# The down projection of nine pairs of row blocks by seven products instead of eight, and the second attention's weights split on ScalarE and VectorE

## The chip, the cores and the metric

The kernel runs on one core of a Trainium2 chip. The metric is the device time of one execution in microseconds, lower is better; the time before is the median of three runs.

## What is computed

Two decoder layers over 1,024 tokens of width 1,024 in float32. The first layer has differential attention, the second stick-breaking attention whose K and V come from the residual stream. Each layer ends in the same feed-forward block, and both of these are what the change touches:

```python
def swiglu(h, w_gate_up, w_down):
    gate, up = jnp.split(h @ w_gate_up, 2, axis=-1)
    return (jax.nn.silu(gate) * up) @ w_down
...
    for layer in range(DEPTH):
        h = rms_norm(x, mix_pre_g[layer])
...
        x = x + rms_norm(m, mix_post_g[layer])
        f = swiglu(rms_norm(x, ffn_pre_g[layer]), ffn_w_gate_up[layer], ffn_w_down[layer])
        x = x + rms_norm(f, ffn_post_g[layer])
```

`D_FF` is 2,816: 22 row blocks of 128, called f = 0 to 21 (`NF`). The gate and up product is 1,024 x 1,024 by 1,024 x 5,632, the down product 1,024 x 2,816 by 2,816 x 1,024.

## The kernel before

**Precision.** Every large product is made of three matmuls of 128x128 by 128x512 (`PASSES`): each operand is kept as a rounded part and a remainder, and high*high, low*high and high*low are summed in one PSUM bank. To split an operand is a copy that rounds (ScalarE, or GpSimd) and a subtraction (GpSimd or VectorE).

**Order of the work.** Coroutines ask for engines and buffers; the class `Weaver` runs them against its own table of costs and writes each engine's instructions down in the order in which they start there. `InOrder` fixes that order per engine. On the chip each engine takes its queue in this order, and each instruction waits for its semaphores, so a late one holds back all behind it on its engine. All DMAs are issued by SP, in one such queue.

**Gate and up.** `phase_ffn.gate_up` already uses seven products instead of eight for each f (`MORD`): `quad` in `loader` loads two 1,024x128 pieces of weights into `raw` tiles, forms five sums or differences on VectorE (`raw<-raw,raw`, `raw<-raw`), rounds seven operands on ScalarE (`w<-raw`) and subtracts on GpSimd (`w<-raw,w`). TensorE does 84 matmuls for each f, against `hT` tiles (four operands) and `hx` tiles (three, which `combine` makes at the phase's start). `take` adds the seven results from PSUM into four `e` tiles: eight additions on VectorE, four copies on ScalarE. `gated` applies silu on ScalarE and multiplies on VectorE (`e<-e`), and `store` writes to DRAM (`act`).

**Down.** `act_in` reads a block back into an `fa` or `fb` tile, rounds it on ScalarE and subtracts on VectorE. `row_job` loads and splits a block of `w_down`, mostly on GpSimd. `down` goes through the groups of `groups_of` (nine of two f and one of four); for each of 8 token blocks m and 2 column halves it does three matmuls per f, then one addition of the bank to an accumulator on VectorE (ScalarE copies in the first group). That is 22 x 16 x 3 = 1,056 matmuls in each layer. From the third token block of the first group on, the copies wait until all of `act` is stored (`all_stored`), since the accumulators lie in the same tiles `e`.

**Weights of the second attention.** While the first layer's feed-forward block runs, `pre_weights` takes 32 weight tiles of the second attention (24 with a gain, `bq`, `bk`, `bv`; then 8 without, `wo`), 128x1024 each, into `tr` tiles: GpSimd multiplies by the gain (`tr<-tr,gB`), ScalarE rounds, GpSimd subtracts (`tr<-tr,tr`), and both parts are stored. It paces itself with a delay of 10 us in the planner's time.

## Time and profile before

| what | us |
|---|---|
| median of three runs (2665.01 to 2668.43) | 2665.74 |
| the profiled execution | 2666.21 |
| its span in the profile | 2664.4 |

The profile is of one execution. Its span runs from the first instruction to the last; 1.8 us lie around it. The first layer's feed-forward block lies at about 606 to 1370 us of the span (gate and up to 1103, down from there), the second layer's at 1983 to the end (down from 2418). In the rows below, names of tiles stand as out<-in, PE is TensorE, DVE VectorE, ACT ScalarE, POOL GpSimd. Matmuls overlap, so the mean length of one is longer than the interval from one to the next.

### The profile page before, as it was taken

The numbers are of one execution on the slowest core, as the hardware profiler recorded it, in microseconds if no ns is written. First come the engines' busy times: TensorE is split into PE (matmuls) and PEld (weight loads), VectorE is DVE, ScalarE is ACT, GpSimd is POOL, SyncE is SP. The second block draws the span as 40 slices with busy tenths as digits, with TensorE's granted clock in tenths as the row PEclk, the third lists the DMA queues.
The fourth block names the chain that finished last, engine by engine and source line by source line (L and its number), as shares of the span: only waits on it lengthen the run. The fifth ranks groups of instructions, "written<-read, shape, count | busy, mean of one in ns | idle before, by whom it ended". The sixth has DMA issues, their size and how long they took to land. (4 is left out here: it accounts for less than half of the span.)

```text
span 2664.4 us, 36544 instructions
## 1 busy us (share of the span) xinstructions
PE 2544.4 (95%) x12771; PEld 2155.9 (81%) x12771; DVE 1824.4 (68%) x3151; ACT 1156.6 (43%) x2542; POOL 922.4 (35%) x769
## 2 busy tenths in 40 slices
PE   8999999896999999899999999999989999999998
PEld 8998999775777877688878888887777888888887
DVE  4767676865766767566668887878777655554667
ACT  4556555644433444310146555556455333332111
POOL 2111111334787878533210000000044545453321
PEclk9999999998999999999999999999999999999999
DMA  6333323442555465542253444434532232324223
GB/s 170 86 80 80 92 76 97 125 166 83 181 171 166 158 199 172 213 166 95 96 197 105 112 117 113 119 104 132 209 121 87 72 95 72 95 72 156 98 102 127
DMA packets 259256, 331.54 MB, mean 124 GB/s; under 512 B 20992, under 2 KB 179072, under 8 KB 259072
## 3 DMA queue, kind: packets, MB, share of 16 engines
q1 hardware_dynamic: 259072, 329.20, 40.1%
q8 instruction: 101, 1.65, 0.3%
q14 instruction: 83, 0.68, 0.1%
HBM read 197.67 MB, written 81.13 MB: 105 GB/s over the span
## 5 line engine op out<-in xcount | busy, mean ns | idle before, releaser
L283 PE MATMUL bank<-hT,w 128*128 128x512 f32 x3264 | 808.6, 398 | 19.6 <-POOL w L283 12.2
L283 PEld LDWEIGHTS bank<-hT,w 128*128 128x128 f32 x3264 | 607.8, 191 | 145.4 <-POOL w L283 15.3
L283 POOL TENSOR_TENSOR w<-raw,w 128x512 fp32r<-128x512 f32 (+1 forms) x343 | 537.2, 1588 | 365.6 <-ACT w L283 309.2
L283 PE MATMUL bank<-hx,w 128*128 128x512 f32 x1584 | 371.1, 392 | 11.0 <-DVE hx L283 8.8
L283 PEld LDWEIGHTS bank<-hx,w 128*128 128x128 f32 x1584 | 298.6, 189 | 76.0 <-DVE hx L283 11.5
L283 DVE TENSOR_TENSOR e<-e,bank 128x512 f32<-128x512 f32 x360 | 237.7, 682 | 168.2 <-PE bank L283 102.1
L283 PE MATMUL bank<-w,hT 128*128 128x384 f32 (+1 forms) x1728 | 346.2, 347 | 3.5 <-DVE v L283 1.1
L283 ACT CAST w<-raw 128x512 fp32r<-128x512 f32 x308 | 185.5, 621 | 337.7 <-DVE raw L283 210.3
L283 PEld LDWEIGHTS bank<-w,hT 128*128 128x128 f32 x1728 | 301.6, 190 | 14.2 <-DVE hT L283 1.5
L283 PE MATMUL bank<-w,fb 128*128 128x512 f32 x1344 | 311.5, 389 | 1.1 <-POOL w L283 1.0
L283 PEld LDWEIGHTS bank<-w,fb 128*128 128x128 f32 x1344 | 252.0, 188 | 54.3 <-POOL w L283 1.5
L283 DVE TENSOR_TENSOR e<-bank,e 128x512 f32<-128x512 f32 x224 | 152.6, 688 | 104.3 <-PE bank L283 102.0
L283 POOL MEMSET atB<- 128x128 f32 x128 | 25.3, 206 | 503.4 <-PE bank L283 498.5
L283 PE MATMUL bank<-ident,tr 128*128 128x128 f32 x1059 | 162.2, 281 | 39.1 <-DVE tr L283 20.2
L283 PE MATMUL bank<-w,fa 128*128 128x512 f32 x768 | 185.5, 396 | 8.5 <-ACT e L283 5.0
L283 PEld LDWEIGHTS bank<-ident,tr 128*128 128x128 f32 x1059 | 129.1, 144 | 70.3 <-DVE tr L283 22.9
L283 PEld LDWEIGHTS bank<-w,fa 128*128 128x128 f32 x768 | 145.7, 191 | 40.8 <-ACT e L283 6.5
L283 POOL TENSOR_TENSOR sm<-sm,nhalf 128x1 f32<-128x1 f32 (+1 forms) x72 | 57.8, 804 | 286.7 <-DVE sm L283 281.6
L283 DVE TENSOR_TENSOR raw<-raw,raw 128x512 f32<-128x512 f32 x132 | 156.8, 1195 | 0.0
L283 POOL TENSOR_SCALAR w<-raw 128x1024 fp32r<-128x1024 f32 x48 | 65.5, 1364 | 261.9 <-PE bank L283 173.6
L283 DVE TENSOR_TENSOR raw<-raw 128x512 f32<-128x512 f32 x88 | 62.4, 743 | 120.4 <-DMA raw<-in_ffn_w_gate_up_dram 117.8
L283 DVE TENSOR_TENSOR_SCAN rB<-rB,zeroB 128x512 f32<-128x512 f32 (+3 forms) x144 | 135.2, 953 | 7.2 <-ACT rB L283 6.0
(209 smaller groups left out, 3640.3 us busy)
## 6 DMA issues: line engine op xcount, KB each, us to landing
raw<-in_ffn_w_gate_up_dram SPq DMA_DIRECT2D x88, 512.0 KB, 5.2
xy<-st SPq DMA_DIRECT2D x192, 128.0 KB, 2.3
act<-e SPq DMA_DIRECT2D x88, 256.0 KB, 4.0
raw<-in_ffn_w_down_dram SPq DMA_DIRECT2D x44, 512.0 KB, 4.1
xyB<-stB SPq DMA_DIRECT2D x176, 128.0 KB, 3.9
fb<-act SPq DMA_DIRECT2D x28, 512.0 KB, 3.9
raw<-in_a_w_qkv_dram SPq DMA_DIRECT2D x96, 128.0 KB, 2.5
tr<-x SPq DMA_DIRECT2D x22, 512.0 KB, 4.3
```

Of the source, the lines that this page charges most:

```text
L283: return tc.keep_in_program_order(f(*a, **k))
```

## The change

For f = 0 to 17 (`ND`), in nine pairs, the down product is made by Strassen's seven products: a pair's two f are the two halves of the inner dimension, the token halves and the column halves are the other two. The pairs go in two groups, of five and of four (`D_GROUPS`); within a group, each of the seven products is summed over the group's pairs in four PSUM banks, and only then added to the accumulators. f = 18 to 21 stay as they were, as the last group.

- `pair_ops` (new) runs while gate and up goes on: five sums or differences of 128x512 on VectorE for each pair, and seven stores to DRAM (`op`) in place of four (`act`).
- `act_in` reads each of the 63 activation operands back into half a tile's width, rounds (ScalarE) and subtracts (VectorE).
- `move_weights` copies 18 blocks of `w_down` from DRAM to DRAM (`wd`). `QuarterJob` loads quarters of them into pieces of the `hT` tiles, which are lent as the last f of gate and up is done with them. `OpJob` makes the 63 weight operands: a sum or difference on VectorE for five of seven (`raw<-hT,hT`), a rounding on ScalarE, a subtraction on GpSimd.
- `down` no longer waits for the pools of its phase before the first matmul; its `evac` does.
- `pre_weights` starts 25 us later, is paced by 13.5 instead of 10 us, and does without GpSimd: for the 24 tiles with a gain eight scaled copies of 128x128 on ScalarE and eight multiply-subtracts of 128x128 on VectorE, for the 8 others a subtraction on VectorE.
- `quad` subtracts one of its seven operands (i = 2) on VectorE.

```diff
 LAMBDA_INIT = 0.8 - 0.6 * math.exp(-0.3 * 0)
 PASSES = ((0, 0), (1, 0), (0, 1))
 MORD = (3, 5, 4, 2, 6, 7, 1)
+DORD = (2, 5, 3, 4, 7, 6, 1)
+D_GROUPS = ((0, 1, 2, 3, 4), (5, 6, 7, 8))
+ND = 18
 NE = 3
...
                 g_ev, g = job.gain()
                 yield g_ev
-                v3 = raw.t.rearrange("p (c n) -> p c n", c=NC)
-                yield POOL(1024, 1.7)
-                pool.tensor_tensor(v3, v3, g.unsqueeze(2).broadcast_to([P, NC, P]), op=ALU.mult)
             h = hi.t.bitcast(F32R)
-            yield ACT(1024)
-            act.copy(h, raw.t)
+            if job.gain is not None:
+                for c in range(NC):
+                    cs = slice(c * P, c * P + P)
+                    yield ACT(P, 1)
+                    act.activation(h[:, cs], raw.t[:, cs], AF.Copy, scale=g[:, c:c + 1])
+                for c in range(NC):
+                    cs = slice(c * P, c * P + P)
+                    yield DVE(P + 58)
+                    dve.scalar_tensor_tensor(raw.t[:, cs], raw.t[:, cs], g[:, c:c + 1], hi.t[:, cs],
+                                             op0=ALU.mult, op1=ALU.subtract)
...
-            yield POOL(1024, 2.2)
-            pool.tensor_tensor(raw.t, raw.t, hi.t, op=ALU.subtract)
...
             sp.dma_start(out=job.view(raw.t), in_=job.src)
             yield delay(2.6)
             W.spawn(work(job, raw, hi), 60, "pre" + job.name)
-            yield delay(10.0)
+            yield delay(13.5)
     def loader():
         queue = []
...
-                pool.tensor_tensor(lo, src, f32(hi), op=ALU.subtract)
+                if i == 2:
+                    yield DVE(512)
+                    dve.tensor_tensor(lo, src, f32(hi), op=ALU.subtract)
+                else:
+                    yield POOL(512, 2.2)
+                    pool.tensor_tensor(lo, src, f32(hi), op=ALU.subtract)
                 job.t[i] = t
                 W.set(job.ev[i])
                 W.set(left)
...
+        def operand(k_, job):
+            yield turn[k_]
+            t = yield acq(S_w)
+            sc = None
+            if len(job.parts) == 2:
+                sc = yield acq(S_raw)
+            W.set(turn[k_ + 1])
+            W.set(job.began)
+            for x in job.parts:
+                yield x.ev
+            src = f32(job.parts[0].t.t)
+            if sc is not None:
+                yield DVE(512)
+                dve.tensor_tensor(sc.t[:, :512], src, f32(job.parts[1].t.t), op=job.op)
+                for x in job.parts:
+                    x.used()
+                src = sc.t[:, :512]
+            hi, lo = t.t[:, :512], t.t[:, 512:]
+            yield ACT(512)
+            act.copy(hi, src)
+            yield POOL(512, 2.2)
+            pool.tensor_tensor(lo, src, f32(hi), op=ALU.subtract)
+            if sc is not None:
+                W.put(sc)
...
-        st.d = [row_job(w_down[layer][f * P:(f + 1) * P], name=f"d{f}") for f in range(NF)]
...
+        for g in D_GROUPS:
+            qs = {p: {} for p in g}
+            for i in DORD:
+                for p in g:
+                    q = qs[p]
+                    if i in (2, 5, 3, 4):
+                        key = {2: 11, 5: 22, 3: 12, 4: 21}[i]
+                        f, ch = 2 * p + key // 10 - 1, key % 10 - 1
+                        q[key] = QuarterJob(st.wd[f][:, ch * 512:(ch + 1) * 512], st.wd_ev[f],
+                                            4 if key in (11, 22) else 2)
+                    parts, op = {2: ((11,), None), 5: ((22,), None), 3: ((12, 22), sub), 4: ((21, 11), sub),
+                                 7: ((21, 22), add), 6: ((11, 12), add), 1: ((11, 22), add)}[i]
+                    st.o[p, i] = OpJob([q[k] for k in parts], op, f"d{p}_{i}", began)
+        st.d = {f: row_job(w_down[layer][f * P:(f + 1) * P], after=began, name=f"d{f}")
+                for f in range(ND, NF)}
...
+        def move_weights():
+            for f in range(ND):
+                yield SP(1.0)
+                sp.dma_start(out=st.wd[f], in_=st.wd_src[f])
+                yield delay(6.0)
+                W.set(st.wd_ev[f])
+                yield delay(6.0)
+
+        def lend_q():
+            def cut(t):
+                return [t[:, k] for k in range(4)]
+
+            yield from W.lend(S_h, S_q, 8, cut, book)
+
...
+            def pair_ops(p):
+                yield pair_ev[p]
+                a11, a21, a12, a22 = gt[2 * p, 0], gt[2 * p, 1], gt[2 * p + 1, 0], gt[2 * p + 1, 1]
+                pr = plan("p.storexf" + nm, 0)
+                keep = [Ref([x], 2) for x in (a11, a22)]
+                for i, x, k in ((3, a11, keep[0]), (4, a22, keep[1])):
+                    W.spawn(store_op(p, i, x.t, k.done), pr, "storeo")
+                for i, x, y in ((2, a21, a22), (5, a11, a12), (1, a11, a22)):
+                    z = yield acq(S_sg, S_tr)
+                    yield DVE(512)
+                    dve.tensor_tensor(z.t[:, :512], x.t, y.t, op=ALU.add)
+                    W.spawn(store_op(p, i, z.t[:, :512], lambda z=z: W.put(z)), pr, "storeo")
+                for i, x, y, k in ((6, a21, a11, keep[0]), (7, a12, a22, keep[1])):
+                    yield DVE(512)
+                    dve.tensor_tensor(x.t, x.t, y.t, op=ALU.subtract)
+                    k.done()
+                    W.spawn(store_op(p, i, x.t, lambda x=x: W.put(x)), pr, "storeo")
...
+            def fin_op(k, t):
+                yield ACT(512)
+                act.copy(t.t[:, :512], f32(t.t[:, 512:]))
+                yield DVE(512)
+                dve.tensor_tensor(t.t[:, 512:], f32(t.t[:, 512:]), f32(t.t[:, :512]), op=ALU.subtract)
+                op_t[k] = t
+                W.set(op_ev[k])
+
+            for k in keys:
+                yield op_stored[k]
+                t = yield acq(S_act)
+                yield SP(0.8)
+                sp.dma_start(out=f32(t.t[:, 512:]), in_=opd[k[0]][k[1]])
+                yield delay(2.4)
+                W.spawn(fin_op(k, t), plan("p.mul" + nm, 1), "opin")
...
+            touched = {r: Ev(4) for r in (0, 1)}
+            evac_done = Ev(4 * 7 * len(D_GROUPS))
+            goes = {1: ((0, 0, 1), (1, 1, 1)), 2: ((1, 0, 1), (1, 1, -1)), 3: ((0, 1, 1), (1, 1, 1)),
+                    4: ((0, 0, 1), (1, 0, 1)), 5: ((0, 0, -1), (0, 1, 1)), 6: ((1, 1, 1),), 7: ((0, 0, 1),)}
+
+            def evac(bk, m, i, first):
+                yield dn_open
+                yield all_stored
+                for r, c, sg in goes[i]:
+                    av = acc[4 * r + m][:, c * 512:(c + 1) * 512]
+                    if first:
+                        yield ACT(512)
+                        if sg > 0:
+                            act.copy(av, bk.t)
+                        else:
+                            act.activation(av, bk.t, AF.Copy, scale=-1.0)
+                    else:
+                        yield touched[r]
+                        yield DVE(512)
+                        dve.tensor_tensor(av, av, bk.t, op=ALU.add if sg > 0 else ALU.subtract)
+                W.put(bk)
+                if first:
+                    W.set(touched[goes[i][0][0]])
+                W.set(evac_done)
+
+            for g in D_GROUPS:
+                for i in DORD:
+                    yield op_ev[g[0], i]
+                    yield st.o[g[0], i].ev
+                    bks = []
+                    for m in range(4):
+                        bks.append((yield acq(B_mm, B_sc, B_tp, B_pv)))
+                    for p in g:
+                        yield op_ev[p, i]
+                        yield st.o[p, i].ev
+                        a, w = op_t[p, i], st.o[p, i].t
+                        for m in range(4):
+                            yield PE(3)
+                            for k, (ah, wh) in enumerate(PASSES):
+                                pe.matmul(bks[m].t, a.t[:, ah * 512 + m * P:ah * 512 + (m + 1) * P],
+                                          w.t[:, wh * 512:(wh + 1) * 512],
+                                          start=(p == g[0] and k == 0), stop=(p == g[-1] and k == 2))
+                        W.put(a, w)
+                    for m in range(4):
+                        W.spawn(evac(bks[m], m, i, g == D_GROUPS[0] and i in (2, 5)), plan("p.acc" + nm, 2), "evac")
+            yield evac_done
+            W.unlend(book)
+            for gr in (list(range(ND, NF)),):
```

**VectorE in the middle of the first layer's gate and up.** `e,bank` rows are the additions from PSUM, `raw` rows the sums of weights, `e<-e` the multiplication after silu; the line is that of the recording helper, 283 before and 286 now. Before, one f and the start of the next:

```order
L283 TENSOR_TENSOR e2_5510<-e2_5510,bank6_139 128x512
L283 TENSOR_TENSOR e2_5510<-e2_5510,bank5_138 128x512
L283 TENSOR_TENSOR raw2_127<-raw0_125,raw2_127 128x512
L283 TENSOR_TENSOR e2_5510<-e2_5510,bank0_133 128x512
L283 TENSOR_TENSOR raw0_125<-raw0_125,raw2_127 128x512
L283 TENSOR_TENSOR e2_5510<-e2_5510,bank0_133 128x512
L283 TENSOR_TENSOR e2_5510<-e2_5510,bank1_134 128x512
L283 TENSOR_TENSOR raw0_125<-raw0_125,raw2_127 128x512
L283 TENSOR_TENSOR e2_5510<-e2_5510,bank4_137 128x512
L283 TENSOR_TENSOR e2_5510<-e2_5510,bank2_135 128x512 x2
L283 TENSOR_TENSOR e2_5510<-e2_5510 128x512 x2
```

In the changed kernel, as far into the stage:

```order
L286 TENSOR_TENSOR w3_119<-raw0_125,w3_119 128x512
L286 TENSOR_TENSOR raw2_127<-raw0_125,raw2_127 128x512
L286 TENSOR_TENSOR e2_5591<-e2_5591,bank5_138 128x512
L286 SCALAR_TENSOR_TENSOR tr1_129<-tr1_129,gB_103,tr0_128 128x128
L286 TENSOR_TENSOR e2_5591<-e2_5591,bank0_133 128x512
L286 TENSOR_TENSOR raw0_125<-raw0_125,raw2_127 128x512
L286 TENSOR_TENSOR e2_5591<-e2_5591,bank0_133 128x512
L286 SCALAR_TENSOR_TENSOR tr1_129<-tr1_129,gB_103,tr0_128 128x128 x2
L286 TENSOR_TENSOR e2_5591<-e2_5591,bank1_134 128x512
L286 TENSOR_TENSOR raw0_125<-raw0_125,raw2_127 128x512
L286 SCALAR_TENSOR_TENSOR tr1_129<-tr1_129,gB_103,tr0_128 128x128 x3
L286 TENSOR_TENSOR e2_5591<-e2_5591,bank4_137 128x512
```

Between the rows of one f there now stand the subtraction `w3<-raw0,w3` of a weight operand and groups of the 128x128 multiply-subtracts of `pre_weights`; the sums of `pair_ops` (`e<-e,e`) follow behind every second f.

**TensorE where the first layer's gate and up ends.** `hT` and `hx` rows are gate and up, rows with `fa` the down projection. Before, its last rows of gate and up and the first of down:

```order
L283 MATMUL bank1_134<-hx4_6094,w8_124 128x512 x2
L283 MATMUL bank1_134<-hx5_6095,w8_124 128x512
L283 MATMUL bank1_134<-hx4_6094,w8_124 128x512
L283 MATMUL bank7_140<-w0_116,fa0_6083 128x512
L283 MATMUL bank7_140<-w0_116,fa1_6084 128x512
L283 MATMUL bank7_140<-w1_117,fa0_6083 128x512
L283 MATMUL bank7_140<-w2_118,fa2_6085 128x512
L283 MATMUL bank7_140<-w2_118,fa3_6086 128x512
L283 MATMUL bank7_140<-w3_119,fa2_6085 128x512
L283 MATMUL bank6_139<-w0_116,fa0_6083 128x512
```

In the changed kernel, within the last f, where its fourth product (bank4) has begun:

```order
L286 MATMUL bank4_137<-hT6_114,w5_121 128x512
L286 MATMUL bank4_137<-hT7_115,w5_121 128x512
L286 MATMUL bank4_137<-hT6_114,w5_121 128x512
L286 MATMUL bank6_139<-w0_116,fa0_6164 128x512 x3
L286 MATMUL bank5_138<-w0_116,fa0_6164 128x512 x3
L286 MATMUL bank0_133<-w0_116,fa0_6164 128x512 x3
L286 MATMUL bank1_134<-w0_116,fa0_6164 128x512 x3
```

And 10 rows on, where gate and up goes on in the same bank:

```order
L286 MATMUL bank5_138<-w3_119,fa3_6167 128x512 x3
L286 MATMUL bank0_133<-w3_119,fa3_6167 128x512 x3
L286 MATMUL bank1_134<-w3_119,fa3_6167 128x512 x3
L286 MATMUL bank4_137<-hT6_114,w5_121 128x512
L286 MATMUL bank4_137<-hT7_115,w5_121 128x512
L286 MATMUL bank4_137<-hT6_114,w5_121 128x512 x2
```

The first four pairs of the first down product, 48 matmuls, now stand inside the last f of gate and up, ahead of three and a half of its seven products. In the second layer they stand behind the last row of gate and up.

**VectorE in the second group of the first layer's down projection.** Rows with `bank` are additions from PSUM, `fa` and `fb` rows the remainders of activation operands, `raw<-hT,hT` the sums of quarters of weights, `tr` a tile of `pre_weights`. Before, in the middle of that layer's down projection:

```order
L283 TENSOR_TENSOR acc0_8956<-bank0_133,acc0_8956 128x512
L283 TENSOR_TENSOR acc0_8956<-bank1_134,acc0_8956 128x512
L283 TENSOR_TENSOR acc1_8957<-bank7_140,acc1_8957 128x512
L283 TENSOR_TENSOR fb1_8961<-fb1_8961,fb0_8960 128x1024
L283 TENSOR_TENSOR fb3_8963<-fb3_8963,fb2_8962 128x1024
L283 TENSOR_TENSOR acc1_8957<-bank6_139,acc1_8957 128x512
L283 TENSOR_TENSOR e0_5508<-bank5_138,e0_5508 128x512
L283 TENSOR_TENSOR e0_5508<-bank0_133,e0_5508 128x512
L283 TENSOR_TENSOR e0_5508<-bank1_134,e0_5508 128x512
```

In the changed kernel:

```order
L286 TENSOR_TENSOR e0_5589<-e0_5589,bank3_136 128x512
L286 TENSOR_TENSOR e0_5589<-e0_5589,bank7_140 128x512
L286 TENSOR_TENSOR e1_5590<-e1_5590,bank4_137 128x512
L286 TENSOR_TENSOR e1_5590<-e1_5590,bank2_135 128x512
L286 TENSOR_TENSOR fb2_9461<-fb2_9461 128x512
L286 TENSOR_TENSOR e2_5591<-e2_5591,bank3_136 128x512
L286 TENSOR_TENSOR e2_5591<-e2_5591,bank7_140 128x512
L286 TENSOR_TENSOR raw2_127<-hT5_113,hT7_115 128x512
L286 TENSOR_TENSOR fb3_9462<-fb3_9462 128x512
L286 TENSOR_TENSOR raw1_126<-hT5_113,hT7_115 128x512
L286 TENSOR_TENSOR raw0_125<-hT5_113,hT7_115 128x512
L286 TENSOR_TENSOR tr2_130<-tr2_130,tr4_132 128x1024
```

Before, sixteen additions stood between one pair of remainders and the next; now eight additions for a product have between them and the next eight four or five remainders of 128x512 and three or four sums of quarters.

## Rows read from the trace of the kernel before

**Rows 1.** The head of the page, and of its DMA issues one row (KB each, us to landing).

```profile
span 2664.4 us, 36544 instructions
...
act<-e SPq DMA_DIRECT2D x88, 256.0 KB, 4.0
```

**Rows 2.** Busy time of each engine by stretch (first column), granted clock, DMA.

```profile
680.00:794.00 114.00, 114.00 (x503) 94.33 (x502) 75.59 (x84) 50.03 (x83) 86.25 (x50) 1.00 0.56 180
794.00:1046.00 252.00, 236.70 (x1011) 192.26 (x1010) 172.72 (x187) 103.14 (x176) 204.08 (x119) 0.97 0.53 174
...
1103.00:1112.00 9.00, 9.00 (x41) 7.42 (x40) 7.36 (x8) 2.84 (x5) 8.13 (x5) 1.00 0.65 223
1112.00:1130.00 18.00, 9.45 (x26) 6.23 (x26) 4.90 (x4) 9.01 (x13) 4.08 (x2) 0.75 0.74 275
...
2018.00:2418.00 400.00, 400.00 (x1767) 331.20 (x1766) 226.18 (x315) 152.28 (x269) 209.32 (x147) 1.00 0.30 92
2418.00:2657.00 239.00, 239.00 (x1056) 197.85 (x1055) 154.78 (x215) 41.61 (x68) 61.56 (x38) 1.00 0.33 113
```

**Rows 3.** Who PE waited for, first layer, 606 to 1130 us.

```profile
PE bank L283 <- POOL w L283: 12.2, 7, 2.5
...
PE bank L283 <- DVE hx L283: 7.6, 3, 2.9
PE bank L283 <- ACT e L283: 5.0, 2, 2.9
PE bank L283 <- ACT acc L283: 3.5, 1, 3.5
...
PE bank L283 <- ACT hx L283: 2.2, 1, 2.2
```

**Rows 4.** The same, second layer, 1983 to 2664 us.

```profile
PE bank L283 <- DVE hx L283: 1.2, 2, 0.7
```

**Rows 5.** Groups by line and form, 680 to 1103 us (first layer's gate and up).

```profile
L283 POOL TENSOR_TENSOR w<-raw,w 128x512 fp32r<-128x512 f32 x140 | 213.6, 1553 | 83.3 <-ACT w L283 83.1
...
L283 DVE TENSOR_TENSOR raw<-raw,raw 128x512 f32<-128x512 f32 x60 | 83.4, 1403 | 0.0
L283 ACT CAST w<-raw 128x512 fp32r<-128x512 f32 x140 | 83.1, 620 | 175.1 <-DMA raw<-in_ffn_w_gate_up_dram 90.9 <-DVE raw L283 82.8 <-PE bank L283 1.1
L283 DVE TENSOR_TENSOR e<-e 128x512 f32<-128x512 f32 x42 | 73.1, 1777 | 18.7 <-ACT e L283 18.2
L283 POOL TENSOR_TENSOR tr<-tr,tr 128x1024 f32<-128x1024 f32 x25 | 64.0, 2562 | 9.3 <-ACT tr L283 9.3
L283 POOL TENSOR_TENSOR tr<-tr,gB 128x1024 f32<-128x1024 f32 x22 | 48.6, 2209 | 0.1
```

**Rows 6.** The same groups, 2018 to 2418 us (second layer's gate and up).

```profile
L283 POOL TENSOR_TENSOR w<-raw,w 128x512 fp32r<-128x512 f32 x140 | 197.5, 1433 | 184.2 <-ACT w L283 174.9 <-PE bank L283 8.0 <-issue 1.1
...
L283 DVE TENSOR_TENSOR e<-e,bank 128x512 f32<-128x512 f32 x170 | 114.4, 685 | 137.1 <-PE bank L283 97.5 <-ACT e L283 39.4
...
L283 DVE TENSOR_TENSOR raw<-raw,raw 128x512 f32<-128x512 f32 x60 | 61.1, 1018 | 0.0
...
L283 DVE TENSOR_TENSOR e<-e 128x512 f32<-128x512 f32 x42 | 29.2, 697 | 2.6 <-ACT e L283 0.7
```

**Rows 7.** Instructions in order of time, from 2203 us.

```profile
2203.12 1.29 POOL L283 TENSOR_TENSOR w<-raw,w 128x512 fp32r<-128x512 f32 x1 [1.33 <-PE bank L283]
2203.31 0.69 DVE L283 TENSOR_TENSOR e<-e,bank 128x512 f32<-128x512 f32 x1 [0.38 <-PE bank L283]
2203.91 1.04 DVE L283 TENSOR_TENSOR raw<-raw,raw 128x512 f32<-128x512 f32 x1
```

**Rows 8.** Groups over the whole span, two-input operations of VectorE with a column of factors.

```profile
L283 DVE SCALAR_TENSOR_TENSOR w<-raw,gA,w 128x384 fp32r<-128x384 f32 x64 | 41.6, 660 | 0.8 <-PE bank L283 0.8
...
L283 DVE SCALAR_TENSOR_TENSOR v<-bank,rsA,v 128x128 fp32r<-128x128 f32 x64 | 21.5, 346 | 29.2 <-ACT v L283 28.9
```

**Rows 9.** Groups, 2424 to 2657 us (second layer's down projection).

```profile
L283 DVE TENSOR_TENSOR fb<-fb,fb 128x1024 fp32r<-128x1024 f32 x13 | 17.5, 1349 | 1.9 <-ACT fb L283 1.9
```

More of the change, by code (lines that the diff above doesn't have):

```diff
@@ L388, in pre_weights @@
         yield ready
+        yield delay(25.0)
         def work(job, raw, hi):
@@ L1667, in gate_up @@
                 ss = []
+                if f < ND and f % 2 == 0:
+                    W.spawn(pair_ops(f // 2), plan("p.silu" + nm, 1), "pairo")
                 job = st.q[f]
```

102 lines of the change are left out of this document (78 added, 24 removed).

## The prediction

> **What bounds the kernel now.** I read the stretches of the span first [rows 2], because the change touches the two feed-forward blocks alone. In the second layer's down projection TensorE is busy for all of 239.00 us with 1,056 matmuls: one every 0.2263 us, at the full granted clock. The second layer's gate and up runs as evenly. There, less time comes only from fewer matmuls. The first layer is another matter. From 794 to 1046 us stand 1,011 matmuls, 228.8 us at that interval, in 252: 23.2 us are lost. At the passage to down, 1103 to 1130, 41 + 26 matmuls make 15.2 us of 27: 11.8 us lost, with a mean granted clock of 0.75 in the second part, so between its two levels of 1.2 and 2.4 GHz. And at the start of gate and up TensorE waited 7.6 + 2.2 us for the `hx` operands [rows 3], where the second layer's whole feed-forward block lost 1.2 us to them [rows 4].
>
> Next I asked who is late. In the first layer's gate and up it is GpSimd's subtraction of weights, 12.2 us in seven waits (the granted clock of that stretch is 0.97 [rows 2]); at the passage it is ScalarE's copies to the accumulators, 5.0 + 3.5 us [rows 3]. GpSimd is late because it shares something with VectorE. Row by row [rows 7]: a GpSimd subtraction begins at 2203.12 and lasts 1.29 us, to 2204.41. An addition from PSUM within it takes its usual 0.69 us. `raw<-raw,raw`, which reads two SBUF operands, begins at 2203.91 and ends at 2204.95, 0.54 us after the subtraction; the same shape takes 0.697 where GpSimd rests (`e<-e` [rows 6]). So the two engines take turns at operations of that kind, and an addition from a bank doesn't take part. Where GpSimd has the long `pre_weights` operations, `e<-e` takes 1.777 us and `raw<-raw,raw` 1.403, against 0.697 and 1.018 in the other layer [rows 5, 6].
>
> The Trainium skill has this as a rule (SBUF — State Buffer, Who interferes with whom): a VectorE instruction with two SBUF inputs contends with a GpSimd instruction that reads SBUF, and the later one is blocked until the first is done. The trace agrees. By the rule, work moved from GpSimd to VectorE frees none of the shared time unless it becomes shorter; what that would make of this change is the third rival.
>
> The bound of the first layer's gate and up can be checked so. In 680 to 1103 us GpSimd's three groups are busy 213.6 + 64.0 + 48.6 = 326 us, and VectorE's two-input operations (60 + 42, and the quads' two other sums for each of 20 f, 40 more) at 0.70 make 99 us: 425 of 423 us [rows 5]. The shared turn is full.
>
> **The change, part by part.**
>
> *Matmuls.* A pair takes 7 x 12 = 84 instead of 96; nine pairs and two layers save 216. At 0.2263 us [rows 2]: **-48.9 us**, certain where TensorE is the bound.
>
> *Start of gate and up.* `pre_weights` begins 25 us later and leaves GpSimd, so the first layer's `hx` subtractions meet what the second layer's meet: 9.8 us of waits fall to 1.2 [rows 3, 4]. **-8**; bounds -10 and 0, the last if VectorE is then late for another reason.
>
> *First layer's gate and up.* One f is 84 matmuls, 19.0 us. GpSimd keeps six subtractions at 1.29 [rows 7]: 7.7 us. VectorE gets, for each f, eight additions at 0.685 [rows 6], 5.5 us; two-input operations 7 + 1 (operand 2) + 2.5 (`pair_ops`) at 0.70, 7.4 us; and eight 128x128 multiply-subtracts. Such a one with both operands in SBUF isn't in the trace: 0.346 us is the same size from PSUM, 0.660 the 384 wide from SBUF [rows 8]; I take 0.35, since it is the size, so 2.8 us (bound 5.3). The shared turn then holds 7.7 + 7.4 + 2.8 = 17.9 of 19.0 us: free at last. But VectorE alone has 15.7 us and on top of it the waiting for GpSimd, between 0 and 6 x 1.29 = 7.7 us. `raw<-raw,raw` in the other layer waits 0.32 each [rows 6]; here more such operations meet each subtraction, so I take 0.55 to 0.85 per subtraction, 3.3 to 5.1 us. That makes 19.0 to 20.8 us for an f: lost 0 to 40 us over 22, taken 18 against 23.2 before. **-5**. Queued behind a late VectorE row are the quad's sums, then ScalarE, GpSimd, TensorE. ScalarE's eight scaled copies are hidden: it was busy 103 of 252 us [rows 2].
>
> *Passage to down, first layer.* Down's first products stand inside the last f. Their weights need a DMA of a quarter after the first product of that f, about 4.0 us for 256 KB (the stores' row [rows 1]), then 0.62 us on ScalarE [rows 5] and 1.29 on GpSimd [rows 7]: 6 us and two hand-overs, against 27 matmuls, 6.1 us, between. A wait of 0 to 4 us, with the rest of gate and up queued behind it. The copies to the accumulators still wait for the last store, but the second product, 60 matmuls or 13.6 us, covers them. 11.8 become 4: **-8** (-12 to 0).
>
> *Down.* 63 operands in 756 matmuls, 171.1 us in each layer. VectorE: 80 additions at 0.685 (16 of 96 go to ScalarE), 54.8; 63 remainders and 45 sums at 0.70, 75.6. A remainder of 1024 took 1.349 [rows 9], so half of it at 0.70 is fair. Sum 130 us, and the waiting for 63 GpSimd subtractions at the same 0.55 to 0.85: 165 to 184 against 171. In the first layer three tiles of `pre_weights` with a gain and some four without come on top, about 14 us. Twelve tiles and nine weight slots of prefetch smooth only a product or two. **+10** in the first layer (0 to 23), **+3** in the second (0 to 13).
>
> *Smaller things.* The second layer's passage, which lost nothing before: **+2** (0 to 5). Its gate and up: VectorE 12.9 us of 19.0 plus waits of 3 to 5, covered: **+1**. `pre_weights` ends later, so its last tiles share `tr` tiles and VectorE with the last transitions of the first layer: **+3** (0 to 8). The DRAM copies and three more stores for a pair lie beside other work, since the 16 DMA engines were busy 0.56 of the time at most in gate and up [rows 2]; without that cover they would delay quads.
>
> Sum: -48.9 - 8 - 5 - 8 + 10 + 3 + 2 + 1 + 3 = **-50.9 us**. The profiled execution took 2666.2 us, 1.8 around its span of 2664.4 [rows 1], and is 0.5 above the median: 2615.3, as a median **2615**.
>
> **Rivals.**
>
> *All waits vanish.* TensorE runs at 0.2263 us throughout both blocks: -48.9 - 8 - 23.2 - 11.8 = -92, so 2574. For it: the shared turn falls below 100% in every stage, and the second layer shows that 209 us of GpSimd in 400 costs TensorE nothing [rows 2]. Against it: VectorE had 226 there, and gets far more now. Chance 0.22.
>
> *VectorE becomes the bound of both stages of the first layer,* at the upper ends: gate and up loses 33 instead of 18, down 23 and 9 instead of 10 and 3. Then -50.9 + 15 + 13 + 6 = -17, so 2649. For it speaks `e<-e` at 1.777, which shows what a blocked VectorE row costs [rows 5]; against it, that the operations of over 2 us are gone from GpSimd. Chance 0.25.
>
> *Slower.* Each GpSimd subtraction blocks VectorE for its whole 1.29 us in the first layer's gate and up: an f takes 15.7 + 7.7 = 23.4 us, 97 us lost instead of 18, and the kernel ends 79 - 50.9 = 28 us slower, 2694. It decides from a loss of 69 us on, 22.1 us for an f. By the rule of the Trainium skill cited above this is the limit of what the move can do. Against it: VectorE's additions from banks fit into GpSimd's time and lie between the other rows in its queue. Chance 0.05.
>
> *No change* by compensating losses near 50 us: 0.03. That the matmuls do not fall in number is excluded by the order of the built program.
>
> **How the numbers follow.** The forecast case (-30 to -75) has 0.45 and gives 2615. Adding most of the first rival (down to 2572) and of the second (up to 2652) leaves out no more than 2 in 10. A measurement of this kernel can tell 0.2%, 5 us, from no change. Faster: 0.45 + 0.22 + 0.25 = 0.92; same 0.03; slower 0.05.
>
> **What would show it.** PE matmuls down by 216. In the first layer's gate and up: no `tr` group on GpSimd, `e<-e` near 0.8 to 1.2 us instead of 1.777, VectorE busy over 0.9 of the time, 19 to 20.5 us for an f, and TensorE's waits on `w` from VectorE's chain instead of GpSimd. `hx` waits near 1 us. In down, 0.2263 us for a matmul in the second layer and a few waits on `w` or `fb` in the first. I am wrong if TensorE waits for DMAs of operands (SP's single queue holds a load back until a tile is free, and all behind it), if the quarters come late at the passage by more than 4 us, or if VectorE's 128x128 rows take far more than 0.35 us.

## The result: 0.8% slower

| | before | after |
|---|---|---|
| median of four runs, us | 2665.38 (2660.93 to 2668.43) | 2685.26 (2683.20 to 2692.36) |
| ratio, 95% interval | | 1.0079 (1.0066 to 1.0092) |

The forecast was 2615 us, faster than before. The head of after's page:

```profile
span 2683.4 us, 37281 instructions
## 1 busy us (share of the span) xinstructions
PE 2519.7 (94%) x12555; PEld 2117.6 (79%) x12555; DVE 2061.2 (77%) x3559; ACT 1288.8 (48%) x2926; POOL 806.8 (30%) x733
```

To find where the time went I cut both spans at four kinds of matmul: the first one of gate and up, the first one of f = 1, the last one of gate and up, and the last one of down. The third column of numbers is a later experiment, e5.

| us of span | before | after | e5 | forecast for after |
|---|---|---|---|---|
| first layer, f = 0 | 73.5 | 64.9 | 61.5 | -8 |
| f = 1 to 21 | 423.4 | 468.0, with 48 matmuls of down (10.9) | 410.5, with the same 48 | -5 (+10.9 for the 48) |
| then to the end of down | 260.5 | 245.0 | 247.8 | -24.4 - 8 + 10 (-10.9 for the 48) |
| attention between | 619.3 | 612.4 | 613.9 | +3 |
| second layer, f = 0 | 35.4 | 35.7 | 36.5 | 0 |
| f = 1 to 21 | 399.6 | 420.2 | 399.6 | +1 |
| then to the end of down | 239.3 | 224.0 | 222.5 | -24.4 + 3 + 2 |

In the first layer down has 1,056 matmuls before, worth 239.0 us at 0.2263, and 948 now, 48 of them inside the last f: 900 left, worth 203.7. So it loses 41.3 us where it lost 21.5. The 48 taken off, f = 1 to 21 take 33.7 us more: 22.3 in f = 1 to 20 (426.9 instead of 404.6) and 11.4 in the last f, where the 48 stand. In the second layer gate and up is 20.6 us longer, and down loses 9.5 us where it lost 0.3. The sum of all (-48.9 - 8.6 + 33.7 + 19.8 - 6.9 + 0.3 + 20.6 + 9.2) is +19.2, and the spans differ by 19.0.

The stretches of after, as in [rows 2] (busy time by engine, granted clock, DMA):

```profile
794.00:1046.00 252.00, 229.63 (x956) 182.62 (x956) 200.89 (x309) 109.37 (x238) 97.14 (x69) 0.97 0.52 171
...
1139.00:1384.00 245.00, 222.21 (x950) 177.11 (x948) 218.23 (x293) 111.43 (x215) 105.90 (x72) 0.97 0.56 190
2032.00:2452.00 420.00, 406.85 (x1764) 331.98 (x1763) 302.94 (x381) 155.54 (x279) 186.69 (x127) 0.99 0.40 129
```

In both layers' gate and up none of the engines that feed TensorE is full: VectorE is busy 201 of 252 us and 303 of 420, GpSimd 97 and 187. Yet TensorE waits. In the second layer its idle time is 13 us of the 20.6; for the rest its matmuls ran longer, at a granted clock of 0.99. An engine's busy time doesn't explain it; a chain does.

**The chain.** TensorE's waits in the second layer (1996 to 2684 us; total, times, longest) name GpSimd first:

```profile
PE bank L286 <- POOL w L286: 8.7, 9, 1.6
```

But GpSimd waits in turn, and so do VectorE and ScalarE. Groups of the second layer's gate and up, 2032 to 2452 us; behind the bar the idle time before them and what ended it:

```profile
L286 DVE TENSOR_TENSOR raw<-raw,raw 128x512 f32<-128x512 f32 x60 | 76.1, 1268 | 0.0
L286 DVE TENSOR_TENSOR raw<-raw 128x512 f32<-128x512 f32 x40 | 37.4, 955 | 92.0 <-DMA raw<-in_ffn_w_gate_up_dram 92.0
...
L286 DVE TENSOR_TENSOR tr<-e,e 128x512 f32<-128x512 f32 x20 | 24.8, 1241 | 0.0
```
```profile
L286 ACT CAST w<-raw 128x512 fp32r<-128x512 f32 x140 | 86.1, 621 | 246.6 <-DVE raw L286 147.1 <-DMA raw<-in_ffn_w_gate_up_dram 99.2
```
```profile
L286 POOL TENSOR_TENSOR w<-raw,w 128x512 fp32r<-128x512 f32 x120 | 178.7, 1502 | 233.4 <-ACT w L286 232.2 <-issue 1.1
```

92 us of VectorE's idle time end with the landing of the weights. In the same stage of before, 2018 to 2418 us, where TensorE lost nothing, it was 32:

```profile
L283 DVE TENSOR_TENSOR raw<-raw 128x512 f32<-128x512 f32 x40 | 26.7, 708 | 32.0 <-DMA raw<-in_ffn_w_gate_up_dram 32.0
```

One f, from its loads to the next f's, in order of time:

```profile
2257.05 1.00 SPq L286 DMA_DIRECT2D raw<-in_ffn_w_gate_up_dram  x2
...
2263.41 0.69 DVE L286 TENSOR_TENSOR raw<-raw 128x512 f32<-128x512 f32 x1 [5.24 <-DMA raw<-in_ffn_w_gate_up_dram]
...
2266.32 1.76 DVE L286 TENSOR_TENSOR tr<-e,e 128x512 f32<-128x512 f32 x1
...
2270.91 0.68 DVE L286 TENSOR_TENSOR raw<-raw,raw 128x512 f32<-128x512 f32 x1
...
2273.31 1.18 DVE L286 TENSOR_TENSOR raw<-raw,raw 128x512 f32<-128x512 f32 x1
...
2275.80 1.33 DVE L286 TENSOR_TENSOR raw<-raw,raw 128x512 f32<-128x512 f32 x1
...
2277.93 1.29 POOL L286 TENSOR_TENSOR w<-raw,w 128x512 fp32r<-128x512 f32 x1 [1.34 <-ACT w L286]
...
2279.24 1.01 SPq L286 DMA_DIRECT2D raw<-in_ffn_w_gate_up_dram  x2
```

`quad` takes three `raw` tiles: two are loaded, the third is scratch for the sums of products 3 and 4. It gives all three back together, after the seventh split, and there are only three. So the next loads are issued when the last GpSimd subtraction is through: 2279.24 is 0.02 us behind its end. One f costs load (6.4 us) plus splitting (15.8), 22.2 us. While it loads, VectorE stands before `raw<-raw` and holds up the additions behind it; after that they run between the quad's own sums. The SP rows of the loads show where the cycle is long (five f in order):

```profile
2113.43 1.03 SPq L286 DMA_DIRECT2D raw<-in_ffn_w_gate_up_dram  x2
...
2132.47 1.06 SPq L286 DMA_DIRECT2D raw<-in_ffn_w_gate_up_dram  x2
...
2154.72 1.02 SPq L286 DMA_DIRECT2D raw<-in_ffn_w_gate_up_dram  x2
...
2173.76 1.00 SPq L286 DMA_DIRECT2D raw<-in_ffn_w_gate_up_dram  x2
...
2196.54 1.01 SPq L286 DMA_DIRECT2D raw<-in_ffn_w_gate_up_dram  x2
```

19.0 and 22.3 or 22.8 us in turn: long where `pair_ops` runs, every second f. Before, from the third f on, one took 18.0 to 19.3 us from issue to issue; it just fitted. In after, f = 1 to 8 of this stage still run at 19.0 on TensorE, most likely from `w` tiles made ahead; then it sinks to the chain's pace.

### The profile page after: what moved, and what is told of

Same layout as the page of the kernel before. It is cut to its first block, busy times and chain, and to the rows that moved or that the text cites. A ratio compares the mean times of both kernels' runs of the same rounds, so it can differ in the third digit from the quotient of the medians.

```text
span 2683.4 us, 37281 instructions
## 1 busy us (share of the span) xinstructions
PE 2519.7 (94%) x12555; PEld 2117.6 (79%) x12555; DVE 2061.2 (77%) x3559; ACT 1288.8 (48%) x2926; POOL 806.8 (30%) x733
## 4 chain that ended last, share of the span: by engine, by line
PE 42%; DVE 29%; DMA 11%; issue 7%; ACT 5%; POOL 4%; SPq 1%; DVEq 0%; ACTq 0%; POOLq 0%
PE bank L286 42%; DVE e L286 7%; DVE raw L286 7%; DVE tr L286 6%; DMA raw<-in_ffn_w_gate_up_dram 5%; POOL w L286 3%; ACT w L286 2%; DVE rB L286 2%; DMA tr<-in_kv_w_dram 2%; DVE atB L286 1%; DVE w L286 1%; SPq L286 1%; DVE fb L286 1%; ACT e L286 1%; DVE fa L286 1%
## 5 line engine op out<-in xcount | busy, mean ns | idle before, releaser
L286 POOL TENSOR_TENSOR w<-raw,w 128x512 fp32r<-128x512 f32 (+1 forms) x363 | 552.9, 1535 | 772.1 <-ACT w L286 698.6
L286 ACT CAST w<-raw 128x512 fp32r<-128x512 f32 x398 | 244.6, 621 | 603.3 <-DVE raw L286 412.1
L286 DVE TENSOR_TENSOR e<-e,bank 128x512 f32<-128x512 f32 x480 | 311.9, 676 | 68.5 <-ACT e L286 49.1
L286 PEld LDWEIGHTS bank<-w,hT 128*128 128x128 f32 x1728 | 300.2, 189 | 15.8 <-DMA w<-prewo 3.5
L286 PE MATMUL bank<-w,fb 128*128 128x512 f32 x1204 | 295.3, 395 | 14.2 <-DVE e L286 5.8
L286 PEld LDWEIGHTS bank<-w,fb 128*128 128x128 f32 x1204 | 227.8, 190 | 66.7 <-DVE fb L286 4.2
L286 DVE TENSOR_TENSOR raw<-raw 128x512 f32<-128x512 f32 x88 | 80.1, 930 | 159.6 <-DMA raw<-in_ffn_w_gate_up_dram 159.6
L286 PEld LDWEIGHTS bank<-w,fa 128*128 128x128 f32 x692 | 133.6, 194 | 47.6 <-POOL w L286 4.4
L286 DVE TENSOR_TENSOR raw<-raw,raw 128x512 f32<-128x512 f32 x132 | 134.4, 1018 | 0.0
L286 ACT CAST atB<-bank 128x512 fp32r<-128x512 f32 (+1 forms) x160 | 84.5, 554 | 88.8 <-PE bank L286 82.7
L286 DVE TENSOR_TENSOR atB<-bank,atB 128x512 fp32r<-128x512 f32 (+1 forms) x160 | 97.6, 629 | 32.9 <-ACT atB L286 32.4
```

Source lines behind the costliest of these rows:

```text
L286: return tc.keep_in_program_order(f(*a, **k))
```

## Experiments

The theory, called the ring in what follows: an f costs load plus splitting in series, since three `raw` tiles circulate, and the change lengthens the splitting. Rivals: VectorE or the shared turn of VectorE and GpSimd has too much work; the DRAM copies slow the loads; `pre_weights` on VectorE does the harm. "f" is TensorE's time from one f to the next, mean over f = 7 to 20; before it is 20.7 us in the first layer and 19.0 in the second, in after 22.2 and 20.4. It comes from one profiled execution, within 3.2 us of the median except for e7 (2669.08, 9.9 above it) and e10 (2627.31, 5.5 below). Before itself had medians of 2664.4 to 2665.6 us next to these runs.

| run | median us | ratio to before, 95% | f, first | f, second |
|---|---|---|---|---|
| e1 loads may use `tr` tiles, both layers | 2750.53 | 1.0321 (1.0303 to 1.0339) | 19.3 | 19.0 |
| e2 DRAM copies early | 2696.42 | 1.0119 (1.0101 to 1.0137) | 22.5 | 20.5 |
| e3 `pre_weights` on GpSimd | 2705.87 | 1.0156 (1.0137 to 1.0175) | 23.4 | 20.3 |
| e4 operand 2 on GpSimd | 2685.94 | 1.0085 (1.0065 to 1.0105) | 22.5 | 19.6 |
| e5 scratch tile given back early | 2606.92 | 0.9795 (0.9778 to 0.9811) | 19.0 | 19.0 |
| e6 as e1, second layer alone | 2667.69 | 1.0011 (1.0001 to 1.0020) | 22.0 | 19.0 |
| e7 without three sums of a pair | 2659.16 | 0.9980 (0.9969 to 0.9991) | 21.8 | 19.5 |
| e8 before, scratch tile given back early | 2632.59 | 0.9885 (0.9870 to 0.9900) | 19.0 | 19.0 |
| e9 e5, pace 10 | 2602.80 | 0.9763 (0.9747 to 0.9779) | 19.0 | 19.0 |
| e10 e5, remainders on GpSimd | 2632.82 | 0.9874 (0.9856 to 0.9891) | 19.0 | 19.0 |
| e11 e5, `pre_weights` on GpSimd | 2619.63 | 0.9824 (0.9809 to 0.9838) | 20.0 | 19.0 |
| e12 e9 and e10 together | 2608.79 | 0.9785 (0.9771 to 0.9800) | 19.0 | 19.0 |

All versions but e2, e3 and e4 hold a second edit, in `to_quad`, which makes the input of gate and up: a block of the second token half waits for the block four before it.

```diff
         yield hid.got[th]
+        if th:
+            yield hid.ev[m - 4]
```

What it does alone can be read in e6's first layer, where nothing else differs from after: 467.6 us for f = 1 to 21 instead of 468.0, so it isn't what shortens an f below.

**e1 and e6: more tiles for the ring.** e1 from f = 3 on in both layers, e6 in the second layer alone, from f = 6 on. The edit of e1:

```diff
-                    raw = yield acq(S_raw)
+                    raw = yield acq(*((S_raw, S_tr) if int(job.name[1:]) >= 3 else (S_raw,)))
...
-                rr.append((yield acq(S_raw)))
+                rr.append((yield acq(*((S_raw, S_tr) if int(job.name[1:]) >= 3 else (S_raw,)))))
```

> The changed kernel; from the fourth f of each layer's gate and up on, the loads of gate and up may also land in the five tr tiles, not only in the three raw tiles, so that the next f's weights are loaded while the last f's are still being split. Theory 1 (the ring): three raw tiles are filled, split and freed together, so an f takes the load (6 to 7 us) plus the splitting (15.8 us in the second layer, 13.2 before), and the added VectorE rows lengthened the splitting. Then the second layer's f falls from 20.4 to 19.0 us and the first layer's from 22.2 to 19.5 to 20.5: 40 to 60 us less, about 2630. Theory 2 (the shared turn of GpSimd and VectorE is full) and theory 4 (the rows of pre_weights fill VectorE): an f still takes 20.4 and 22 us, no change beyond 10 us. Theory 3 (the added DMA traffic lengthens the loads): as theory 1 in this run.

> After, with the loads of gate and up's weights allowed to land in the five tr tiles as well, in the second layer alone and from its seventh f on, when nothing else there uses them. Theory A: the second layer's f after f 7 falls from 20.4 to 19.0 us, its gate and up ends 18 to 20 us earlier, and the first layer and the attention between are as in after; 2665 us (2660 to 2671). Theory B: 20.4 us stay, 2685 us. If the time given back in gate and up is lost again in the second down projection, 2675 to 2685 us with an f of 19.0.

With more tiles f falls to 19.3 and 19.0 with the same number of instructions on every engine. e1 missed its 2630 us by far, since `pre_weights` lives on the same `tr` tiles: from the end of the first down to the second gate and up it takes 758 us instead of 612. TensorE waits there for weights of `pre_weights` read back from DRAM, 61 of the 146 us; the others stay open:

```profile
PE bank L286 <- DMA w<-prewo: 36.2, 8, 18.8
PE bank L286 <- DMA hT<-prewo: 25.1, 8, 4.4
```

e6 harms nobody: its second gate and up takes 399.6 us, as before, and the kernel wins 17.6 on after.

**e2: the copies out of the way.** They run during attention.

```diff
-            W.spawn(move_weights(), 60, "movew")
...
         def move_weights():
+            if nm == "B":
+                yield phase_done["ffnA"]
...
+        W.spawn(move_weights(), 60, "movew")
         W.spawn(gate_up(), plan("p.gu" + nm, 12), "gu" + nm)
```

> The changed kernel with the 18 copies of w_down from DRAM to DRAM made during the attention ahead instead of during gate and up. Theory 3 (DMA traffic): the load of a quad, 6.3 to 7.2 us in the second layer, falls to the 5.8 of before, and an f to 19.0 to 19.5 and 21 us: about 30 us less. Theory 1 (the ring, with VectorE's rows as what became longer): the load becomes up to 1 us shorter, the splitting stays at 15.8: 5 to 15 us less. Theories 2 and 4: within 5 us.

f stays as in after: the copies aren't what makes it late. As a whole e2 is 11 us slower than after, most of it in the attention (618.5 us), where copies now lie, and in the first gate and up.

**e3 and e4: work back to GpSimd.**

```diff
-                    act.activation(h[:, cs], raw.t[:, cs], AF.Copy, scale=g[:, c:c + 1])
...
-                    dve.scalar_tensor_tensor(raw.t[:, cs], raw.t[:, cs], g[:, c:c + 1], hi.t[:, cs],
-                                             op0=ALU.mult, op1=ALU.subtract)
...
+                pool.tensor_tensor(v3, v3, g.unsqueeze(2).broadcast_to([P, NC, P]), op=ALU.mult)
...
+            pool.tensor_tensor(raw.t, raw.t, hi.t, op=ALU.subtract)
```

> The changed kernel with the work of pre_weights on GpSimd again (multiplication and subtraction of 128x1024), at the new start and pace. Theory 4 (the 128x128 rows on VectorE are what slows the first layer): the first layer's f falls from 22.2 to about 20.4, the second layer's value, the total by 30 us. Theory 2 (the shared turn): GpSimd's long operations fill the turn again, 7.7 + 5.7 + 7.4 = 20.8 us of each f, and the f stays at 21 to 22.5: within 15 us. Theory 1 says in between: VectorE has 4 us less in each f but waits up to 2 us for a long operation; 21 us, about 15 us less.

```diff
-                if i == 2:
-                    yield DVE(512)
-                    dve.tensor_tensor(lo, src, f32(hi), op=ALU.subtract)
-                else:
-                    yield POOL(512, 2.2)
-                    pool.tensor_tensor(lo, src, f32(hi), op=ALU.subtract)
+                yield POOL(512, 2.2)
+                pool.tensor_tensor(lo, src, f32(hi), op=ALU.subtract)
```

> The changed kernel with all seven subtractions of a quad on GpSimd again. Theory 1: VectorE has one row of 0.8 us less between a quad's sums, but GpSimd's row of subtractions gets 1.3 us longer; the second layer's f moves by less than 0.7 us either way, the total within 15 us. Theory 2 (the shared turn is the bound): the turn holds 0.6 us more for each f, so about 0.6 us slower an f, 20 to 25 us in total. Theories 3 and 4: no change.

e3 is 21 us slower than after, so leaving GpSimd helped; its 23.4 us for an f lie above what any of the theories had. e4 gains 0.8 us of f in the second layer and loses 0.3 in the first: no difference in all.

**e5 and e8: the ring shortened without another tile.** Scratch goes back once products 3 and 4 are split, and the up block, which 3 and 5 read, is loaded first, into that tile. e8 is the same on the kernel before.

```diff
+            yield job.ev[3]
+            yield job.ev[4]
+            W.put(rs)
             yield left
-            W.put(ra, rb, rs)
+            W.put(rb, ra)
...
-                for src in job.srcs:
+                for src in reversed(job.srcs):
...
-                W.spawn(quad(k, job, *rr), plan("p.splitg", 20), "quad" + job.name)
+                W.spawn(quad(k, job, rr[1], rr[0], rr[2]), plan("p.splitg", 20), "quad" + job.name)
```

> After, with one thing changed in the splitting of a quad: the scratch tile (sums 3 and 4) is given back as soon as products 3 and 4 are split, and the up block, which products 3 and 5 read, is loaded into it first; the gate block follows when the other two tiles come free. No tile is added. Theory A (load and splitting of the three raw tiles stand in series): one of the two loads then runs beside the last splits, and the first two splits run beside the other; 20 f after f 7 fall from 22.2 to 19.3-20.5 us in the first layer and from 20.4 to 19.0-19.3 in the second, and nobody else loses a tile; 2640 us (2630 to 2660). Theory B (VectorE simply has too much to do for an f): 22.2 and 20.4 stay, 2685 us. If the time falls but only in the second layer (2665 us), the first layer has a second limit.

> The kernel before with the same early release of the scratch tile as in the run on after. Theory A: the second layer stays at 19.0 us (TensorE bounds it); in the first layer the 20.7 us for an f after f 7 are load plus splitting too, so it falls to 19.2-20.0; 2650 us (2643 to 2657). The reading of the prediction (GpSimd's and VectorE's shared turn is full in the first layer of before, whatever the tiles): 20.7 stays, 2665 us.

e5 and e8 are better than their forecasts, e5 with the same number of instructions for TensorE, VectorE, ScalarE and GpSimd as after. One f in it:

```profile
2207.01 4.66 POOL L286 TENSOR_TENSOR w<-raw,w 128x512 fp32r<-128x512 f32 x3 [2.74 <-ACT w L286]
...
2211.69 8.11 SPq L286 DMA_DIRECT2D raw<-in_ffn_w_gate_up_dram  x2
...
2220.16 1.30 POOL L286 TENSOR_TENSOR w<-raw,w 128x512 fp32r<-128x512 f32 x1 [1.43 <-ACT w L286]
...
2224.71 0.69 DVE L286 TENSOR_TENSOR raw<-raw 128x512 f32<-128x512 f32 x1
```

The first load is issued at 2211.69, 0.02 us after the third subtraction, the second 7.7 us later, and `raw<-raw` no longer waits for a DMA. In the whole of the second layer's gate and up, 1976 to 2375 us:

```profile
L286 DVE TENSOR_TENSOR raw<-raw 128x512 f32<-128x512 f32 x40 | 48.0, 1207 | 0.0
```

The first layer's 794 to 1046 us, e5 and then e8:

```profile
794.00:1046.00 252.00, 252.00 (x1114) 208.66 (x1113) 235.99 (x363) 130.68 (x291) 121.76 (x82) 1.00 0.64 208
```
```profile
794.00:1046.00 252.00, 252.00 (x1113) 208.66 (x1113) 180.20 (x199) 116.23 (x195) 208.73 (x126) 1.00 0.62 196
```

TensorE waits for nothing in either. The 23 us that before lost here [rows 2] were the ring as well. VectorE's row says the same, before (680 to 1103 us) and in e8 (678 to 1078):

```profile
L283 DVE TENSOR_TENSOR raw<-raw 128x512 f32<-128x512 f32 x40 | 29.3, 764 | 81.7 <-DMA raw<-in_ffn_w_gate_up_dram 79.1 <-POOL tr L283 2.6
```
```profile
L283 DVE TENSOR_TENSOR raw<-raw 128x512 f32<-128x512 f32 x40 | 47.9, 1220 | 3.1 <-DMA raw<-in_ffn_w_gate_up_dram 3.0
```

Between e5 and e8, with the scratch tile given back early in both, the change is worth 25.7 us.

**e7: VectorE's rows in the splitting.**

```diff
-                    z = yield acq(S_sg, S_tr)
-                    yield DVE(512)
-                    dve.tensor_tensor(z.t[:, :512], x.t, y.t, op=ALU.add)
-                    W.spawn(store_op(p, i, z.t[:, :512], lambda z=z: W.put(z)), pr, "storeo")
+                    W.spawn(store_op(p, i, y.t, lambda: None), pr, "storeo")
```

> After, with the three sums of a pair's activations (operands 2, 5 and 1) left out: an existing tile is stored in the place of each, so that these operands hold another value; the two differences, all stores and all products stay. It takes 27 VectorE rows of two SBUF operands from each layer's gate and up, 1.5 for an f. Theory A (VectorE's rows between the quad's own sums lengthen the splitting, and with it the chain): f falls by 0.8 to 1.5 us in both layers, to 20.7-21.4 and 19.0-19.6; 2655 us (2645 to 2670). Theory B' (the pair sums lie in VectorE's idle time while the load runs): 22.2 and 20.4 stay, 2680 to 2685 us.

f falls by 0.9 us of the 1.4 in the second layer, but by only 0.4 of 22.2 in the first. The median fell by 26.1 us against after, the profiled execution by 16.1 only, so its f may be somewhat high. In the second layer these sums are most of what lengthened the splitting. What else did in the first stays open: the rows of `pre_weights` are a candidate, but e3, which takes them off VectorE, puts 128x1024 operations on GpSimd in their place, and its f rises.

**e9 to e12: what is left, on top of e5.** e9 and e10 are the two edits; e11 is e3's edit, e12 both of the first.

```diff
-            yield delay(13.5)
+            yield delay(10.0)
```
```diff
-                yield DVE(512)
-                dve.tensor_tensor(t.t[:, 512:], f32(t.t[:, 512:]), f32(t.t[:, :512]), op=ALU.subtract)
+                yield POOL(512, 2.2)
+                pool.tensor_tensor(t.t[:, 512:], f32(t.t[:, 512:]), f32(t.t[:, :512]), op=ALU.subtract)
```

> The scratch-early version of after (2606.9 us), with pre_weights' tiles issued every 10 us of the plan, as in before, instead of every 13.5; its start 25 us later stays. In the version the first layer's down needs 247.8 us from the end of gate and up for 900 matmuls worth 203.7, VectorE is busy 20 of 20 us in much of it, and 24 multiply-subtracts of 128x128 (21.7 us) and seven remainders of 128x1024 (11.8 us) of pre_weights lie there. Theory A (VectorE is the bound of the first layer's down, and pre_weights' last tiles are what makes it so): they move into gate and up, the down's loss of 44 us falls by 20 to 33, f stays at 19.0 to 19.4; 2583 us (2574 to 2595). Theory B (gate and up has no room for them): f of 20 to 21 us and 2600 to 2625. Theory C (the down is late for another reason, such as the operands' loads): 2607.

> The scratch-early version of after (2606.9 us), with the 63 remainders of the loaded activation operands (fb<-fb and fa<-fa of 128x512) of each layer's down on GpSimd instead of VectorE. They were 54 us of VectorE in the first layer's down, and VectorE was busy 224 of 260 us there, GpSimd 109. Theory A (VectorE's sum is the bound): the first layer's down falls from 247.8 to 215-230 us and the second's loss from 8 to 3 us; 2585 us (2573 to 2595). Theory B (the turn that the two engines take at SBUF operands is the bound, so it does not matter who does the subtraction, and GpSimd needs twice the time for one): GpSimd then holds 126 subtractions of 1.3 to 1.75 us, 160 to 220 us of some 205, down stays at 245 us or grows to 265; 2607 to 2640 us.

> The scratch-early version of after (2606.9 us), with pre_weights' multiplications and subtractions on GpSimd again as in before, in the new pace. Theory A (the move away from GpSimd is a gain by itself, as the start of gate and up showed): the first hx operands wait again, f in the first layer rises to 19.3-20.5; 2625 us (2612 to 2645). Theory B (with the tiles free in time GpSimd has room for it, as it had in the run of before with the scratch tile early, at 19.0 us): 2607 us, or some 10 to 20 us less, since VectorE, which bounds the first layer's down, is freed of 33 us there: 2587 to 2607.

> The scratch-early version of after (2606.9 us) with both the earlier pace of pre_weights and the remainders of the activation operands on GpSimd. If VectorE's sum bounds the first layer's down, both help but not in full together: 2575 us (2565 to 2590), with the first layer's down at 210 to 220 us. If the shared turn bounds it, 2585 to 2620, no better than the better of the two alone.

e9: f is 19.0 us, as its theory A had it, but the first down falls from 247.8 to 232.5 us only, so `pre_weights`' last tiles are 15 us of its loss. The attention after it grows from 613.9 to 620.0 us and the second down by 2, and 4 us of gain are left, outside the forecast of 2574 to 2595. At 2602.80 us it is the fastest version.

e10: VectorE was relieved of 54 us, and the first down won 6 (247.8 to 241.7), while the second lost 11 (222.5 to 233.4). VectorE's sums in e5 and in e10, 1077 to 1326 us:

```profile
L286 DVE TENSOR_TENSOR raw<-hT,hT 128x512 f32<-128x512 f32 x43 | 38.3, 912 | 1.2 <-POOL w L286 1.2
```
```profile
L286 DVE TENSOR_TENSOR raw<-hT,hT 128x512 f32<-128x512 f32 x43 | 59.2, 1403 | 27.0 <-POOL w L286 27.0
```

GpSimd in e10:

```profile
L286 POOL TENSOR_TENSOR w<-raw,w 128x512 fp32r<-128x512 f32 (+1 forms) x47 | 76.7, 1638 | 3.1 <-ACT w L286 2.9
L286 POOL TENSOR_TENSOR fb<-fb 128x512 fp32r<-128x512 f32 x39 | 55.3, 1428 | 6.8 <-ACT fb L286 6.3
```

Two things came in place of the 54 us. The sums took 1.40 us each instead of 0.91: the turn. And VectorE stood 27 us until GpSimd's subtraction gave back the `raw` tile that the next sum is written to (`operand` in the change): a ring again, now of sum, rounding and GpSimd's subtraction. Which of the two bounds the down isn't separated. Theory B of that run, the turn, had the down at 245 to 265 us and narrowly missed; the total lies in its range for another reason, since 18.8 of the 20.3 us by which the profile is longer than e5's lie in the attention behind the first down (632.7 instead of 613.9), which no theory spoke of and which stays open.

e11: the start of gate and up stays short (61.6 us), but f rises to 20.0, and the run is 13 us slower than e5: within its theory A. e12 is no better than e9.

## Why the prediction was wrong

**Matmuls, -48.9.** Right: 216 fewer. **Start of gate and up, -8.** Right: -8.6.

**First layer's gate and up, -5, and the second's, +1: the step that failed.** It compared VectorE's and GpSimd's sums with the 19.0 us of an f, as if the work of one f could lie beside that of the next. The three `raw` tiles forbid that: load and splitting are one chain, in the second layer 18.0 to 19.3 us before and some 22 after where a pair's sums fall in. The terms measured +22.3 (f = 1 to 20) and +20.6. The row that said so stood in the argument's own list: ScalarE's `w<-raw` waited 90.9 us for DMA `raw` in the first layer [rows 5]. I read its mean and not its idle time. The row of the wait named GpSimd, and I took the last link for the cause. Two of the prediction's own signs of being wrong came: a load held back until a tile is free, though it showed at VectorE and ScalarE and not as a wait of TensorE for a DMA, and 128x128 rows far over 0.35 us. The Trainium skill has the symptom (Perfetto Trace Analysis, Optimization Strategy): bubbles that repeat on the engine that should be full can mean that there is no room for the next tile. The runs agree: e6's additional tiles bring f to 19.0 us; and e5 shows that giving one back earlier does the same without more room.

**"The shared turn is full."** Wrong as the bound. The 326 us of GpSimd contain its own waiting: its subtraction counts 1.553 us there [rows 5], and 1.29 where it came first [rows 7]. e8 does that work, with GpSimd's three groups at 324 us, in 400 us, and TensorE waits for none of it.

**Passage and down, first layer, -8 and +10.** Forecast together at +2, they measured +31.2: 11.4 in the last f and 19.8 behind it. The last f, with the first products of down in it, was to wait 4 us. TensorE's waits in 1045 to 1139 us, and the stretch of that f:

```profile
PE bank L286 <- ACT w L286: 7.0, 3, 3.2
PE bank L286 <- DVE e L286: 2.5, 1, 2.5
```
```profile
1100.00:1138.00 38.00, 32.25 (x124) 25.27 (x124) 23.74 (x37) 15.61 (x35) 18.49 (x15) 0.87 0.78 266
```

The granted clock was 0.87. e5 loses nothing in that f (29.7 us for its 132 matmuls), while e1, whose other f have come down, loses as much as after (41.7 us), so what holds it isn't shown.

In the down behind it VectorE was busy 218 of 245 us. Its 128x128 rows were taken at 0.35 us. The groups of after, 671 to 1112 us and 1139 to 1384:

```profile
L286 DVE SCALAR_TENSOR_TENSOR tr<-tr,gB,tr 128x128 f32<-128x128 f32 x160 | 88.5, 592 | 0.0
```
```profile
L286 DVE SCALAR_TENSOR_TENSOR tr<-tr,gB,tr 128x128 f32<-128x128 f32 x24 | 21.7, 948 | 0.0
```

Sorted by whether a GpSimd instruction overlaps them, 70 of the 160 have none and take 0.34 us, as the estimate had it, and 90 take 0.79; in the down 8 take 0.34 and 16 take 1.25. In order of time, from e5:

```profile
1134.42 0.34 DVE L286 SCALAR_TENSOR_TENSOR tr<-tr,gB,tr 128x128 f32<-128x128 f32 x1
...
1134.68 0.68 DVE L286 TENSOR_TENSOR raw<-hT,hT 128x512 f32<-128x512 f32 x1
1134.68 1.83 POOL L286 TENSOR_TENSOR w<-raw,w 128x512 fp32r<-128x512 f32 x1 [1.34 <-ACT w L286]
1135.28 1.38 DVE L286 SCALAR_TENSOR_TENSOR tr<-tr,gB,tr 128x128 f32<-128x128 f32 x1
```

The first is done as GpSimd begins. At 1134.68 both engines begin: VectorE's sum takes its 0.68 us and GpSimd's subtraction 1.83 instead of 1.29. The 128x128 row begun within that subtraction ends 0.15 us after it. `pre_weights`' tiles were put at 14 us in the down and took 32 (these 21.7 and 10.7 for those without a gain); the remainders `fb<-fb` took 0.91 instead of 0.70. So the waiting on the turn was under-sized; e9 shows that `pre_weights`' tiles, their waiting included, are 15 us of the down's loss. How the remaining 29 us of e9's first down divide between turn, operands' loads and passage stays open.

**Second down and passage, +3 and +2.** 9.2 measured, the same mis-sizing at less weight. **Transitions, +3.** -6.9 measured: the attention became shorter; why stays open.

**The slower rival** (0.05) came near by luck: 2694 us forecast, 2685 measured. It had the place right, the first layer's gate and up, and its 22.1 us for an f came for f = 7 to 20 (22.2). But f = 1 to 5 run at 19.0, so f = 1 to 20 lose 46 us against e5, short of its 69, and the rest came from stages that it didn't name. Its mechanism, each GpSimd subtraction holding up VectorE for its whole length, isn't the bound: e5 keeps every subtraction and runs at 19.0.

The Trainium skill's rule on the turn (SBUF — State Buffer, Who interferes with whom), that a VectorE instruction with two SBUF inputs contends with a GpSimd instruction that reads SBUF, agrees with e10: with the remainders moved to GpSimd, VectorE's sums of two SBUF operands grew from 0.91 to 1.40 us.

## What to carry to other kernels

Beside each engine's sum put the period of each ring of tiles: load, plus everything up to the last reader that gives the tile back. When it is near the stage's pace, work put between its steps can cost time though the engine has room: VectorE was busy 303 of 420 us. Read the idle column for "DMA" on the engines that feed the late one, and give a tile back when its own last reader is done: here 2.9% of after (e5) and 1.2% of before (e8) for a few lines.
